# Moving the fourth recurrent head ahead of keys, values and queries in a hybrid encoder layer

## The chip, the cores and the metric

The kernel computes one encoder layer on one core of a Trainium2 chip. Its engines each run their own queue of instructions in order and meet at semaphores: TensorE (PE; its weight loads are shown as PEld), VectorE (DVE), ScalarE (ACT), GpSimd (POOL), and SyncE (SP), which issues transfers. The metric is the time of one execution in microseconds on the device (us); lower is better. Every time in this document is in us unless it says otherwise.

## The reference, cut to what matters

The layer has 512 tokens of width 1024 and a memory of 256 tokens. The change lies in the first sub-layer alone, which mixes tokens by two head groups side by side:

```
h = rmsnorm(x, pre_mix_g)
aq, ak, av, hq, hf_fwd, hf_bwd, hi, hg = split_columns(h @ w_in, (512, 128, 128, 512, 512, 512, 512, 512))
aq = rmsnorm(aq per head, q_norm_g);  ak = rmsnorm(ak per head, k_norm_g)
att = axial_gqa_attention(apply_rope(aq), apply_rope(ak), av)      # 8 heads of 64, 2 of keys and values
rec = hgrn2_group(hq, hf_fwd, hf_bwd, hi, hg, lb, hg_out_norm_g)   # 4 heads, gated scan in both directions
x = x + rmsnorm(concat(att, rec) @ w_out, post_mix_g)
m = rmsnorm(mem, mem_norm_g)
x = x + rmsnorm(memory_cross_attention(rmsnorm(x, pre_x_g), m, wq, wkv, wo), post_x_g)
x = x + rmsnorm(conv_ffn(rmsnorm(x, pre_ffn_g), ...), post_ffn_g)
```

Attention is softmax(q k / 8) v for each of the 8 heads. A recurrent head runs a scan with a forget gate forwards and backwards over the tokens, adds both, normalizes the sum and multiplies it by silu(hg).

## The kernel before, in words

**Products.** Every large product is made of three fp32r products of a high and a low part (`mm3`: hi·hi, hi·lo, lo·hi; lines 149, 150 and 151). So each operand has to be split into `hi` and `lo` first: ACT casts (line 103 or 126) and DVE subtracts (line 104).

**Weights.** The host packs all weights into 132 units of 128x1024. SP loads a unit into one of two `raw` buffers, ACT casts it into `wh` (line 126 for units 7 to 41), and the remainder `wl` follows in one of three ways: by DVE; by ACT and an accumulating transfer issued by POOL (units 7 to 27); or by a POOL multiplication (line 130) and such a transfer (line 131, units 28 to 41). `wh` and `wl` have four buffers each and a unit is asked for three units ahead, so that the cast of unit u+4 waits until PE has done the last product with unit u.

**The recurrent heads.** For head h, `hgrn_in(h)` projects three units (the query and two gates) feature-major into bank "b", each 24 products of 512 columns, and DVE scales each result (line 451). `hgrn_core(h)` then runs the scan as a chain of levels: PE makes four small products of a level (line 516), ACT and DVE (line 542) scale the keys and queries in place, and the next level needs that. At its end come the outputs (lines 554 to 556), their squares (ACT, line 560), a reciprocal root of four values per row by POOL (lines 167, 168), the gated scaling by DVE (line 566), four transposes on PE (line 570) and a split into the mixing operand.

**Queries.** The query projection leaves four blocks of 128 tokens in the banks "s" and "o". For each, `put_qn` squares (ACT, line 593), sums (DVE, line 595), makes eight reciprocal roots per row (POOL, lines 167, 168 and 597), turns by the rotary tables (DVE, lines 602 to 606), scales (line 607), splits (ACT line 103, DVE line 104), and transposes on PE (line 637, four transposes twice). A block's work is called a job below.

**Order.** Generators yield after each piece of work, and `weave` advances the one that is behind by its share; a tile scheduler then sets each engine's final order. First stage: `mix_projections` (gates, the memory's norm, heads 1 and 2, the memory's transposes `mem_turn`, keys and values, queries, head 3) with a share of 100 beside the cores of heads 0, 1 and 2 with a share of 53. The four jobs on the queries are called between the projections of head 3. Second stage: the core of head 3, `attention` (32 steps of scores, softmax, transposes and, every second step, products with the values, line 733) and `attention_filler`: the memory's keys as eight chunks of 24 products of 256 columns (units 26 to 33, one unit each), its values (units 34 to 37), and the first half of the output projection (units 38 to 41), in which the last unit waits for the last attention heads.

Of the kernel before, what the change touches and what calls it, by code (L numbers as in the profile page):

```python
# [31 lines left out]
TURN_STEP, MEM_TURN, UP_TURN = 0, (0, 4), (0, 2)  # L32
NEG_SCALAR = frozenset(range(7, 28))
NEG_POOL = frozenset(range(28, 42))
CORE_SHARE = 53.0
WARM, SPREAD_STEP = 4, 2
LEVELS = (1, 2, 4, 8, 16, 32, 64)
ASK = 3
# [35 lines left out]
def layer(tc, io, out):  # L74
# [18 lines left out]
    def big(shape, dt=F32):  # L93
        return b8.tile(shape, dt, name="big", tag="big")
# [366 lines left out]
                                       op0=ALU.mult, op1=ALU.mult)  # L461
        sg_box.append(b)

    def hgrn_in(h, between=()):
        qk = big([P, 2, 2, T])
        tt = big([P, 2048])
        q = tmp2(tag="tq")

        def put_q(z):
            nc.scalar.activation(q, z, ACT.Sigmoid)  # L470
            nc.vector.tensor_mul(q, z, q)

        def put_f(d):
            def put(z):
                f = tt[:, d * T:(d + 1) * T]
                k = qk[:, 1, d, :]
                nc.scalar.activation(f, z, ACT.Sigmoid)
                nc.scalar.activation(k, z, ACT.Sigmoid, scale=-1.0)
                nc.scalar.activation(f, f, ACT.Identity, scale=oml[:, d, h:h + 1], bias=lb[:, d, h:h + 1])
                nc.vector.scalar_tensor_tensor(out=qk[:, 0, 1 - d, :], in0=f, scalar=oml[:, d, h:h + 1], in1=q,  # L480
                                               op0=ALU.mult, op1=ALU.mult)
            return put

        for put in (put_q, put_f(0), put_f(1)):
            yield from proj_fm(hT, T, "b", scaled(put))
            for job in between[:2]:
                job()
            between = between[2:]
        heads[h] = (q, qk, tt)

    def hgrn_core(h):
# [118 lines left out]
    def put_kv(b, z):  # L610
        if "rope" not in qkv:
            qkv["rope"] = rope_tables()
            qkv["kT"] = big([P, 4, T], F32R)
            qkv["vv"] = const.tile([P, NB, 2, 2, 64], F32R, name="vv")
            qkv["qT"] = [big([P, 4, T], F32R) for _ in range(2)]
        vv = qkv["vv"]
        split_scaled(vv[:, b, :, 0, :], vv[:, b, :, 1, :], z[:, 128:256].rearrange("p (h d) -> p h d", h=2), r[:, b:b + 1])
        kr = norm_rope(z[:, 0:128], 2, 1, b)
        kd = tmp2((P, 2, 2, 2, 64), F32R)
        nc.scalar.copy(kd[:, :, 0], kr[:, :, None, :].to_broadcast([P, 2, 2, 64]))  # L620
        nc.vector.tensor_tensor(out=kd[:, :, 1], in0=kr[:, :, None, :].to_broadcast([P, 2, 2, 64]),
                                in1=kd[:, :, 0].bitcast(F32), op=ALU.subtract)
        o = bank("b").rearrange("p (k n) -> p k n", k=4)
        kd4 = kd.rearrange("p a b c d -> p (a b) (c d)")
        for i in range(4):
            nc.tensor.transpose(o[:, i, :].bitcast(F32R), kd4[:, i, :], ident_r)
        nc.scalar.copy(qkv["kT"][:, :, blk(b)], o)

    def put_qn(b, z):
        qr = norm_rope(z, 8, 0, b)  # L630
        qs = tmp4([P, 8, 2, 64], F32R)
        split(qs[:, :, 0, :], qs[:, :, 1, :], qr)
        q3 = qs.rearrange("p h a d -> p h (a d)")
        for g in range(2):
            o = bank("so"[g]).rearrange("p (k n) -> p k n", k=4)
            for i in range(4):
                nc.tensor.transpose(o[:, i, :].bitcast(F32R), q3[:, 4 * g + i, :], ident_r)
            if g:
                nc.vector.tensor_copy(qkv["qT"][g][:, :, blk(b)], o)
            else:  # L640
                nc.scalar.copy(qkv["qT"][g][:, :, blk(b)], o)
# [20 lines left out]
    def mix_projections():  # L662
        yield from proj_tm(hT, tm_tags, put_sg)
        mem_norm()
        yield from hgrn_in(1)
        yield from hgrn_in(2)
        mem_turn()
        yield from proj_tm(hT, tm_tags, put_kv, 256)
        late = []
        yield from proj_tm(hT, tm_tags, lambda b, z: late.append(lambda: put_qn(b, z)))  # L670
        yield from hgrn_in(3, late)

    def cores():
        for h in range(3):
            yield from hgrn_core(h)

    for i, _ in enumerate(hgrn_in(0)):
        if i == SPREAD_STEP:
            spread_r()
    weave((mix_projections(), 100.0), (cores(), CORE_SHARE))  # L680

    kT, vv, qT = qkv["kT"], qkv["vv"], qkv["qT"]

    scaled = [0]

# [18 lines left out]
    def attention():  # L704
        probs, pts, atts = {}, {}, {}

        def scores(i):
            h, qb = divmod(i, 4)
            s = bank("s")
            for c in range(2):  # L710
                nc.tensor.matmul(s, qT[h // 4][:, h % 4, blk(qb)], kT[:, 2 * (h // 4) + c, :],  # L711
                                 start=c == 0, stop=c == 1)
            probs[i] = softmax(s, 1, 512)

# [29 lines left out]
                att_done[0] += 1  # L744

        n = 8 * NB
        for i in range(n + 4):
            if i < n:
                scores(i)
            if 2 <= i <= n + 1:  # L750
# [25 lines left out]
        yield from proj_tm(kv["m"], "bb", put_vx(0))  # L776
        kv["y0"] = yield from res_first(mix, MIX_ORDER, lambda j: rec_done[0] == 4 if j >= 2 else att_done[0] >= 2 * j + 2)

    weave((hgrn_core(3), 22.0), (attention(), 42.0), (attention_filler(), 52.0))

    x = load_x()
    g_post, g_pre = gains("post_mix_g", "pre_x_g")
# [153 lines left out]
def pack_weights(w_in, w_xkv, w_out, w_xq, w_xo, w_up, w_down):  # L936
# [16 lines left out]
    tm(w_in, 2816)  # L953
    head(1)
    head(2)
    kv = w_in[:, 512:768].reshape(KC, P, 256)
    for j in range(2):
        units.append(kv[4 * j:4 * j + 4].transpose(1, 0, 2).reshape(P, 1024))
    tm(w_in, 0)
    head(3)  # L960
    for c in range(8):
        fm(w_xkv, c * P)
    tm(w_xkv, 1024)
# [59 lines left out]
```

## Time and profile before

| | |
|---|---|
| Median of three runs | 844.49 |
| Lowest, highest | 843.57, 844.58 |
| Profiled execution, time | 846.16 |
| Profiled execution, span | 844.3 |
| PE busy in the span | 828.5 (98%) |
| DVE, ACT, POOL busy | 488.2 (58%), 427.7 (51%), 102.4 (12%) |
| Mean granted PE clock | 0.996 |

The span is the stretch that the profiler shows on the core; 1.86 of the profiled execution's time lies outside it. Start times are from the span's start. "Granted clock" is the share of full speed at which PE was let run. In a row of the timeline stand start, duration, engine, line, operation, what it writes and reads, how many instructions are joined in the row (x4), and in brackets how long the engine stood idle before it and which engine's result ended that. The durations of pipelined products overlap: the distance between two starts says what one costs. A busy PE may still run its products further apart than it could, so that distances between starts also show waits that the idle time doesn't list.

The stage that the change touches goes from about 50 to 320. The query projection ends at 182, head 3's projections fill 182 to 198.7, and the memory's keys begin there.

### The profile page before, as it was taken

What the parts mean: (1) busy time and instruction counts of PE and PEld (TensorE: products, weight loads), DVE (VectorE), ACT (ScalarE), POOL (GpSimd) and SP (SyncE); (2) the same over time, 40 slices, a digit from 0 to 9 for tenths busy, and PEclk for the clock granted to TensorE, in tenths of its full rate; (3) what the DMA queues carried; (4) which work ended last, traced back from release to release, by engine and by line L of the source; (5) the groups of instructions that cost most, each with busy time, mean ns of one, the idle gap of its engine ahead of it and who ended that gap; (6) DMA issues with size and microseconds to landing.
All of it is one profiled execution on the core that took longest, in us unless ns stands there. A gap on an engine that the chain in (4) does not pass through costs nothing.

```text
span 844.3 us, 11078 instructions
## 1 busy us (share of the span) xinstructions
PE 828.5 (98%) x4304; PEld 703.4 (83%) x4304; DVE 488.2 (58%) x759; ACT 427.7 (51%) x736; POOL 102.4 (12%) x163
## 2 busy tenths in 40 slices
PE   9999999997999999999999999999999999999996
PEld 7888888886999888888888998888888888888885
DVE  5364677619996775854444865555555557722224
ACT  6576656546898874645443553333333335511121
POOL 0212202317223201300001300000000000000001
PEclk9999999999999999999999999999999999999999
DMA  9687754477477643341302333322222222322312
GB/s 322 182 202 203 159 112 113 101 153 181 98 157 162 149 131 119 101 160 65 125 25 75 99 126 101 101 95 88 93 99 99 100 101 94 101 88 94 99 50 100
DMA packets 29796, 101.81 MB, mean 121 GB/s; under 512 B 3952, under 2 KB 4464, under 8 KB 29744
## 3 DMA queue, kind: packets, MB, share of 16 engines
q1 hardware_dynamic: 22752, 77.38, 27.3%
q0 software_dynamic: 6272, 22.81, 14.7%
q10 hardware_dynamic: 720, 0.92, 0.3%
q8 instruction: 34, 0.56, 0.3%
q14 instruction: 18, 0.15, 0.1%
HBM read 99.00 MB, written 2.10 MB: 120 GB/s over the span
## 4 chain that ended last, share of the span: by engine, by line
PE 91%; DVE 3%; ACT 2%; DMA 2%; POOL 1%; issue 1%; POOLq 0%; DVEq 0%; ACTq 0%
PE ps_b L149 9%; PE ps_b L150 9%; PE ps_b L151 9%; PE ps_s L151 6%; PE ps_s L149 6%; PE ps_s L150 6%; PE ps_o L149 6%; PE ps_o L151 6%; PE ps_o L150 6%; PE ps_c L149 4%; PE ps_c L150 4%; PE ps_c L151 4%; PE ps_c L516 3%; PE ps_o L733 2%; PE ps_s L711 2%; PE ps_o L721 2%
## 5 line engine op out<-in xcount | busy, mean ns | idle before, releaser
L104 DVE TENSOR_TENSOR wl<-raw,wh 128x1024 fp32r<-128x1024 f32 x93 | 113.8, 1224 | 199.9 <-ACT wh L103 199.8
L103 ACT CAST wh<-raw 128x1024 fp32r<-128x1024 f32 x93 | 97.9, 1053 | 206.2 <-PE ps_o L151 71.4
L149 PE MATMUL ps_b<-big,wh 128*128 128x512 f32 (+1 forms) x320 | 118.6, 371 | 2.1 <-DVE tmp L451 2.1
L150 PE MATMUL ps_b<-big,wh 128*128 128x512 f32 (+1 forms) x320 | 117.5, 367 | 0.0
L151 PE MATMUL ps_b<-big,wl 128*128 128x512 f32 (+1 forms) x320 | 117.3, 367 | 0.0
L149 PEld LDWEIGHTS ps_b<-big,wh 128*128 128x128 f32 x320 | 61.0, 191 | 11.3 <-DVE tmp L451 2.3
L151 PEld LDWEIGHTS ps_b<-big,wl 128*128 128x128 f32 x320 | 60.9, 190 | 9.3
L150 PEld LDWEIGHTS ps_b<-big,wh 128*128 128x128 f32 x320 | 60.9, 190 | 9.0
L177 POOL TENSOR_SCALAR small<-small 128x1 f32<-128x1 f32 x40 | 13.9, 348 | 440.7 <-ACT tmp L208 421.8
L149 PE MATMUL ps_s<-wh,big 128*128 128x512 f32 (+1 forms) x140 | 54.1, 387 | 0.0
L151 PE MATMUL ps_s<-wh,big 128*128 128x512 f32 (+1 forms) x140 | 53.3, 381 | 0.0
L150 PE MATMUL ps_s<-wl,big 128*128 128x512 f32 (+1 forms) x140 | 53.0, 379 | 0.0
L542 DVE TENSOR_TENSOR big<-big 128x512 f32<-128x512 f32 x64 | 47.9, 755 | 8.4 <-PE ps_c L516 4.6
L126 ACT CAST wh<-raw 128x1024 fp32r<-128x1024 f32 x35 | 36.7, 1048 | 30.3 <-PE ps_o L151 16.1
L149 PE MATMUL ps_o<-wh,big 128*128 128x512 f32 (+1 forms) x124 | 47.9, 386 | 0.0
L151 PE MATMUL ps_o<-wh,big 128*128 128x512 f32 (+1 forms) x124 | 46.7, 377 | 0.0
L150 PE MATMUL ps_o<-wl,big 128*128 128x512 f32 (+1 forms) x124 | 46.7, 377 | 0.0
L131 POOL DMA_DIRECT2D wl<-in_w_dram x35 | 31.2, 892 | 112.9 <-ACT wl L128 103.3
L104 DVE TENSOR_TENSOR big<-ps_o,big 128x512 fp32r<-128x512 f32 x52 | 35.7, 688 | 15.1 <-ACT big L103 14.9
L103 ACT CAST big<-ps_o 128x512 fp32r<-128x512 f32 x52 | 30.3, 586 | 19.6 <-PE ps_o L830 7.5
L149 PE MATMUL ps_b<-wh,big 128*128 128x512 f32 x92 | 36.7, 399 | 0.0
L150 PE MATMUL ps_b<-wl,big 128*128 128x512 f32 x92 | 36.2, 393 | 0.0
(248 smaller groups left out, 1949.2 us busy)
## 6 DMA issues: line engine op xcount, KB each, us to landing
raw<-in_w_dram SPq DMA_DIRECT2D x131, 512.0 KB, 3.3
wl<-in_w_dram POOLq DMA_DIRECT2D x35, 512.0 KB, 5.6
big<-in_x_dram SPq DMA_DIRECT2D x8, 512.0 KB, 7.5
big<-in_xt_dram SPq DMA_DIRECT2D x3, 512.0 KB, 7.8
big<-in_mem_dram POOLq DMA_DIRECT2D x2, 512.0 KB, 8.2
out_dram<-big SPq DMA_DIRECT2D x4, 256.0 KB, 2.0
out_dram<-big ACTq DMA_DIRECT2D x3, 256.0 KB, 2.0
big<-in_xt_dram SPq DMA_DIRECT2D x2, 256.0 KB, 3.5
```

The source lines that it names most:

```text
L103: nc.scalar.copy(hi, src)
L104: (eng or nc.vector).tensor_sub(lo, src, hi.bitcast(F32))
L126: nc.scalar.copy(wh, raw)
L131: nc.gpsimd.dma_start(wl, io["w"][i], accum_op=ALU.add)
L149: nc.tensor.matmul(o, a[0], b[0], start=start, stop=False)
L150: nc.tensor.matmul(o, a[0], b[1], start=False, stop=False)
L151: last_mm[0] = nc.tensor.matmul(o, a[1], b[0], start=False, stop=stop).ins
L516: nc.tensor.matmul(o[:, b, :], kc[:, blk(b)], pat(qk, b * P, [[2 * m, P // (2 * m)], [T + m, 2], [1, m]]), start=True, stop=True)
L542: nc.vector.tensor_tensor(out=c, in0=c, in1=pat(tt, toff + off, [[2, npair], [gap, 2], [0, m]]), op=ALU.mult)
L711: nc.tensor.matmul(s, qT[h // 4][:, h % 4, blk(qb)], kT[:, 2 * (h // 4) + c, :], start=c == 0, stop=c == 1)
L721: nc.tensor.transpose(o[:, c, :], e[:, 0, blk(c)], ident)
L733: nc.tensor.matmul(o, vv[:, c, h // 4].rearrange("p a d -> p (a d)"), pt[:, j, c, :], start=c + j == 0, stop=c == 3 and j == 1)
```

## The change

Four things are moved. `mix_projections` projects head 3 right after heads 1 and 2, ahead of `mem_turn`, keys, values and queries, and the host packs the units in that order (units 17 to 19 are head 3's now, 20 and 21 keys and values, 22 to 25 queries; 26 and above are as they were). All four cores are woven beside the projections, with a share of 60 in place of 53, and so the second stage has none. The jobs on the queries become a stream of their own in the second stage (a share of 110, 3 per job), beside attention (47 in place of 42) and its filler (52). And attention begins with a lead of 5 on its stream, and each of its first four steps waits until as many jobs have been asked for. The transposes of a job go to bank "c" (the cores' bank) in place of "s" and "o", and the tiles for the transposed queries are taken when the first job runs. Lines of the changed kernel stand one lower than before up to `hgrn_in`'s head, then two higher (542 is now 540, 566 is 564), and `put_qn`'s transposes are line 636.

```diff
--- before.py
+++ after.py
@@ -32,7 +32,8 @@
 TURN_STEP, MEM_TURN, UP_TURN = 0, (0, 4), (0, 2)
 NEG_SCALAR = frozenset(range(7, 28))
 NEG_POOL = frozenset(range(28, 42))
-CORE_SHARE = 53.0
+CORE_SHARE = 60.0
+Q_STEP, ATT_LEAD = 3.0, 5.0
 WARM, SPREAD_STEP = 4, 2
 LEVELS = (1, 2, 4, 8, 16, 32, 64)
 ASK = 3
@@ -461,7 +462,7 @@
                                        op0=ALU.mult, op1=ALU.mult)
         sg_box.append(b)
 
-    def hgrn_in(h, between=()):
+    def hgrn_in(h):
         qk = big([P, 2, 2, T])
         tt = big([P, 2048])
         q = tmp2(tag="tq")
@@ -483,9 +484,6 @@
 
         for put in (put_q, put_f(0), put_f(1)):
             yield from proj_fm(hT, T, "b", scaled(put))
-            for job in between[:2]:
-                job()
-            between = between[2:]
         heads[h] = (q, qk, tt)
 
     def hgrn_core(h):
@@ -612,7 +610,6 @@
             qkv["rope"] = rope_tables()
             qkv["kT"] = big([P, 4, T], F32R)
             qkv["vv"] = const.tile([P, NB, 2, 2, 64], F32R, name="vv")
-            qkv["qT"] = [big([P, 4, T], F32R) for _ in range(2)]
         vv = qkv["vv"]
         split_scaled(vv[:, b, :, 0, :], vv[:, b, :, 1, :], z[:, 128:256].rearrange("p (h d) -> p h d", h=2), r[:, b:b + 1])
         kr = norm_rope(z[:, 0:128], 2, 1, b)
@@ -627,12 +624,14 @@
         nc.scalar.copy(qkv["kT"][:, :, blk(b)], o)
 
     def put_qn(b, z):
+        if "qT" not in qkv:
+            qkv["qT"] = [big([P, 4, T], F32R) for _ in range(2)]
         qr = norm_rope(z, 8, 0, b)
         qs = tmp4([P, 8, 2, 64], F32R)
         split(qs[:, :, 0, :], qs[:, :, 1, :], qr)
         q3 = qs.rearrange("p h a d -> p h (a d)")
         for g in range(2):
-            o = bank("so"[g]).rearrange("p (k n) -> p k n", k=4)
+            o = bank("c").rearrange("p (k n) -> p k n", k=4)
             for i in range(4):
                 nc.tensor.transpose(o[:, i, :].bitcast(F32R), q3[:, 4 * g + i, :], ident_r)
             if g:
@@ -664,22 +663,29 @@
         mem_norm()
         yield from hgrn_in(1)
         yield from hgrn_in(2)
+        yield from hgrn_in(3)
         mem_turn()
         yield from proj_tm(hT, tm_tags, put_kv, 256)
-        late = []
         yield from proj_tm(hT, tm_tags, lambda b, z: late.append(lambda: put_qn(b, z)))
-        yield from hgrn_in(3, late)
+
+    late, asked_q = [], [0]
 
     def cores():
-        for h in range(3):
+        for h in range(4):
             yield from hgrn_core(h)
+
+    def query_jobs():
+        while late:
+            late.pop(0)()
+            asked_q[0] += 1
+            yield Q_STEP
 
     for i, _ in enumerate(hgrn_in(0)):
         if i == SPREAD_STEP:
             spread_r()
     weave((mix_projections(), 100.0), (cores(), CORE_SHARE))
 
-    kT, vv, qT = qkv["kT"], qkv["vv"], qkv["qT"]
+    kT, vv = qkv["kT"], qkv["vv"]
 
     scaled = [0]
 
@@ -708,7 +714,7 @@
             h, qb = divmod(i, 4)
             s = bank("s")
             for c in range(2):
-                nc.tensor.matmul(s, qT[h // 4][:, h % 4, blk(qb)], kT[:, 2 * (h // 4) + c, :],
+                nc.tensor.matmul(s, qkv["qT"][h // 4][:, h % 4, blk(qb)], kT[:, 2 * (h // 4) + c, :],
                                  start=c == 0, stop=c == 1)
             probs[i] = softmax(s, 1, 512)
 
@@ -744,7 +750,10 @@
                 att_done[0] += 1
 
         n = 8 * NB
+        yield ATT_LEAD
         for i in range(n + 4):
+            while asked_q[0] < min(NB, i + 1):
+                yield None
             if i < n:
                 scores(i)
             if 2 <= i <= n + 1:
@@ -776,7 +785,7 @@
         yield from proj_tm(kv["m"], "bb", put_vx(0))
         kv["y0"] = yield from res_first(mix, MIX_ORDER, lambda j: rec_done[0] == 4 if j >= 2 else att_done[0] >= 2 * j + 2)
 
-    weave((hgrn_core(3), 22.0), (attention(), 42.0), (attention_filler(), 52.0))
+    weave((query_jobs(), 110.0), (attention(), 47.0), (attention_filler(), 52.0))
 
     x = load_x()
     g_post, g_pre = gains("post_mix_g", "pre_x_g")
@@ -953,11 +962,11 @@
     tm(w_in, 2816)
     head(1)
     head(2)
+    head(3)
     kv = w_in[:, 512:768].reshape(KC, P, 256)
     for j in range(2):
         units.append(kv[4 * j:4 * j + 4].transpose(1, 0, 2).reshape(P, 1024))
     tm(w_in, 0)
-    head(3)
     for c in range(8):
         fm(w_xkv, c * P)
     tm(w_xkv, 1024)
```

**PE where the second stage begins.** Around a job's transposes (line 637 before, 636 after; `tmp4` is the split query block, `ps_b` a chunk of the memory's keys, `wh` and `wl` its unit). Before, the third job's:

```order
L149 MATMUL ps_b_1888<-big_1110,wh_1647 128x256
L150 MATMUL ps_b_1888<-big_1111,wh_1647 128x256
L151 MATMUL ps_b_1888<-big_1110,wl_1648 128x256
L637 MATMUL ps_s_1790<-ident_r_262,tmp4_1787 128x128 x4
L637 MATMUL ps_o_1796<-ident_r_262,tmp4_1787 128x128 x4
L149 MATMUL ps_b_1942<-big_1110,wh_1739 128x256
L150 MATMUL ps_b_1942<-big_1111,wh_1739 128x256
```

After, the fourth job's:

```order
L150 MATMUL ps_b_2129<-big_1365,wh_1928 128x256
L151 MATMUL ps_b_2129<-big_1366,wh_1928 128x256
L152 MATMUL ps_b_2129<-big_1365,wl_1929 128x256
L636 MATMUL ps_c_2057<-ident_r_262,tmp4_2054 128x128 x4
L636 MATMUL ps_c_2063<-ident_r_262,tmp4_2054 128x128 x4
L150 MATMUL ps_b_2197<-big_1365,wh_1990 128x256
L151 MATMUL ps_b_2197<-big_1366,wh_1990 128x256
L717 MATMUL ps_s_2143<-big_1513,big_1894 128x512 x2
```

Before, the first job's transposes begin within head 3's last projection, the third's stand between the chunks of units 26 and 27 (above), and the fourth's within unit 27's. After, the first job's stand behind 27 products of the chunks of units 26 and 27, and those of the fourth (above) behind the four chunks of units 26 to 29, 96 products, with the first two pairs of score products (line 717) among them.

**POOL around the same jobs.** Lines 167, 168 and 597 (168, 169 and 595 after) are a job's reciprocal root, 130 and 131 (131 and 132) a unit's multiplication and transfer. Before, the third and fourth job:

```order
L167 TENSOR_SCALAR small_1778<-small_1776 128x8
L168 TENSOR_TENSOR small_1778<-small_1778,nhalf_82 128x8
L597 TENSOR_SCALAR small_1778<-small_1778,rx_276 128x8
L130 TENSOR_SCALAR wl_1892<-wh_1891 128x1024
L131 DMA wl_1892<-in_w_dram 128x1024
L167 TENSOR_SCALAR small_1806<-small_1804 128x8
L168 TENSOR_TENSOR small_1806<-small_1806,nhalf_82 128x8
L597 TENSOR_SCALAR small_1806<-small_1806,rx_276 128x8
L130 TENSOR_SCALAR wl_1946<-wh_1945 128x1024
L131 DMA wl_1946<-in_w_dram 128x1024
```

After:

```order
L168 TENSOR_SCALAR small_2005<-small_2003 128x8
L169 TENSOR_TENSOR small_2005<-small_2005,nhalf_82 128x8
L131 TENSOR_SCALAR wl_1991<-wh_1990 128x1024
L595 TENSOR_SCALAR small_2005<-small_2005,rx_276 128x8
L132 DMA wl_1991<-in_w_dram 128x1024
L131 TENSOR_SCALAR wl_2081<-wh_2080 128x1024
L168 TENSOR_SCALAR small_2045<-small_2043 128x8
L132 DMA wl_2081<-in_w_dram 128x1024
L169 TENSOR_TENSOR small_2045<-small_2045,nhalf_82 128x8
L595 TENSOR_SCALAR small_2045<-small_2045,rx_276 128x8
```

The number of instructions is the same; the third and fourth jobs' three now have multiplications and transfers of the units between them.

**PE at the end of head 1's core.** Line 556 (554 after) is the last product of the outputs, 570 (568) the transposes of the scaled outputs, 506 (504) the first product of the next core. Before, with the memory's transposes (line 193) and the keys and values (`ps_s`) between:

```order
L193 MATMUL ps_b_1126<-ident_79,big_720 128x128 x4
L151 MATMUL ps_s_1140<-wh_872,big_109 128x256
L570 MATMUL ps_c_1167<-ident_79,tmp2_1063 128x128 x4
L506 MATMUL ps_c_1178<-tmp2_868,tmp2_1175 128x128 x4
L149 MATMUL ps_s_1141<-wh_872,big_107 128x256
```

After, with head 3's projections between:

```order
L152 MATMUL ps_b_1083<-big_108,wl_832 128x512
L150 MATMUL ps_b_1083<-big_108,wh_831 128x512
L568 MATMUL ps_c_1076<-ident_79,tmp2_1025 128x128
L151 MATMUL ps_b_1083<-big_110,wh_831 128x512
L568 MATMUL ps_c_1076<-ident_79,tmp2_1025 128x128 x2
L152 MATMUL ps_b_1083<-big_108,wl_832 128x512
L568 MATMUL ps_c_1076<-ident_79,tmp2_1025 128x128
L150 MATMUL ps_b_1124<-big_107,wh_872 128x512
```

Between the last output product and the first transpose there stand 23 products and three groups of four memory transposes before, and 9 products after.

**DVE at the same place.** Line 566 (564) is the gated scaling, 451 (452) the scaling of a projection, 480 (481) a gate, 502 (500) the first instruction of the next core, 109 the split of the transposed outputs, 104 the split of the memory's transposes. Before:

```order
L542 TENSOR_TENSOR big_739<-big_739,big_740 128x2x2x128 x2
L480 SCALAR_TENSOR_TENSOR big_866<-big_867,oml_307,tmp2_868 128x512
L566 SCALAR_TENSOR_TENSOR tmp2_1063<-ps_c_1050,small_1069,big_653 128x128 x4
L451 TENSOR_TENSOR tmp2_1104<-ps_b_1072,big_292 128x512
L104 TENSOR_TENSOR big_1111<-ps_b_1112,big_1110 128x4x128
L502 SCALAR_TENSOR_TENSOR tmp2_1175<-big_866,oml_307,tmp2_1175 128x512
L480 SCALAR_TENSOR_TENSOR big_866<-big_867,oml_307,tmp2_868 128x512
```

After:

```order
L540 TENSOR_TENSOR big_739<-big_739,big_740 128x2x2x128 x2
L481 SCALAR_TENSOR_TENSOR big_866<-big_867,oml_307,tmp2_868 128x512
L564 SCALAR_TENSOR_TENSOR tmp2_1025<-ps_c_1012,small_1031,big_659 128x128 x4
L452 TENSOR_TENSOR tmp2_1115<-ps_b_1083,big_292 128x512
L109 SCALAR_TENSOR_TENSOR big_771<-ps_c_1076,og_296,big_771 128x512
L500 SCALAR_TENSOR_TENSOR tmp2_1139<-big_866,oml_307,tmp2_1139 128x512
L481 SCALAR_TENSOR_TENSOR big_866<-big_867,oml_307,tmp2_868 128x512
```

The next core's first instruction now stands behind the split of the outputs of the core before.

## The prediction

> **What bounds the kernel now.** I read the page's busy times first, then PE's waits and the stretches of the stage that changes, then its timeline.
>
> ```profile
> PE 828.5 (98%) x4304; PEld 703.4 (83%) x4304; DVE 488.2 (58%) x759; ACT 427.7 (51%) x736; POOL 102.4 (12%) x163
> ```
>
> PE bounds the span, so an edit is worth what it takes from, or adds to, PE's gaps. In PE's waits between 100 and 260 (us in total, times, longest) and in two stretches of 25 (PE first, granted clock third from the end):
>
> ```profile
> PE ps_s L637 <- DVE tmp L104: 2.5, 2, 1.9
> PE ps_b L149 <- DVE tmp L451: 2.1, 1, 2.1
> PE ps_c L516 <- DVE big L542: 1.2, 2, 1.0
> PE ps_b L193 <- DVE tmp L451: 0.8, 1, 0.8
> PE ps_o L733 <- DVE big L104: 0.5, 1, 0.5
> ...
> 125.00:150.00 25.00, 23.11 (x179) 21.87 (x178) 18.63 (x42) 15.73 (x33) 4.89 (x9) 1.00 0.42 96
> 200.00:225.00 25.00, 20.97 (x152) 19.98 (x153) 23.21 (x41) 20.26 (x37) 8.86 (x11) 0.93 0.52 114
> ```
>
> The worst stretch is 200 to 225, where the query jobs, head 3's core and the start of attention all want DVE (23.21 of 25). The timeline of PE there, and the clock in steps of 3:
>
> ```profile
> 181.99 0.39 PE L149 MATMUL ps_b<-big,wh 128*128 128x512 f32 x1
> ...
> 203.21 0.28 PE L150 MATMUL ps_b<-big,wh 128*128 128x256 f32 x1
> 203.33 0.28 PE L151 MATMUL ps_b<-big,wl 128*128 128x256 f32 x1
> 205.50 0.54 PE L637 MATMUL ps_s<-ident_r,tmp 128*128 128x128 f32 x4 [1.89 <-DVE tmp L104]
> 208.50 0.38 PE L149 MATMUL ps_b<-big,wh 128*128 128x256 f32 x1 [2.12 <-DVE tmp L451]
> 209.10 0.42 PE L149 MATMUL ps_b<-big,wh 128*128 128x256 f32 x1
> 209.32 0.41 PE L150 MATMUL ps_b<-big,wh 128*128 128x256 f32 x1
> ...
> 206.00:209.00 3.00, 0.88 (x8) 0.74 (x7) 3.00 (x6) 1.11 (x2) 1.98 (x3) 0.96 0.99 239
> 209.00:212.00 3.00, 3.00 (x16) 3.00 (x16) 2.38 (x5) 2.59 (x5) 0.00 (x0) 0.50 0.95 182
> ```
>
> A 256-column product costs 0.12 (203.21 to 203.33), at the half clock that follows the two waits 0.22 (209.10 to 209.32). Some 15 go at half clock: 1.4 lost.
>
> **What the change takes away.** The first two rows of the waits and the last all hang on DVE's load in this stage; head 3's core leaves it, and nothing is projected beside the jobs. That is 2.5 + 2.1 + 0.5 = 5.1. By distances between starts the two long waits are 0.3 larger than their brackets, the short one ahead of them 0.1. With the clock's 1.4: −6.9.
>
> **What the jobs cost in their new place.** They now start at the end of the query projection (t = 0, 181.99 in the old trace), and PE has only the memory's keys to fill with. One job's chain before, and the price of its links:
>
> ```profile
> 189.07 0.69 DVE L595 TENSOR_REDUCE small<-tmp 128x8 f32<-128x512 f32 x1 [0.75 <-ACT tmp L593]
> ...
> 189.85 0.57 POOL L167 TENSOR_SCALAR small<-small 128x8 f32<-128x8 f32 x1 [4.35 <-DVE small L595]
> ...
> 193.81 0.19 POOL L167 TENSOR_SCALAR small<-small 128x8 f32<-128x8 f32 x1
> 194.08 1.66 POOL L168 TENSOR_TENSOR small<-small,nhalf 128x8 f32<-128x8 f32 x1
> 195.85 0.63 POOL L597 TENSOR_SCALAR small<-small,rx 128x8 f32<-128x8 f32 x1
> 196.44 1.07 POOL L130 TENSOR_SCALAR wl<-wh 128x1024 fp32r<-128x1024 f32 x1
> 197.81 0.92 POOL L131 DMA_DIRECT2D wl<-in_w_dram  x1 [0.30 <-POOL wl L130]
> 198.80 0.19 POOL L167 TENSOR_SCALAR small<-small 128x8 f32<-128x8 f32 x1
> ...
> L607 DVE TENSOR_TENSOR tmp<-tmp,small x4: 674/927/1533, 193.3 to 208.4; 128x512 f32<-128x512 f32 x4
> ...
> 182.19 1.05 ACT L126 CAST wh<-raw 128x1024 fp32r<-128x1024 f32 x1 [3.21 <-PE ps_o L151]
> ...
> wl<-in_w_dram POOLq DMA_DIRECT2D x7, 512.0 KB, 5.9
> ```
>
> A job's three POOL instructions take 2.63 (193.81 to 196.44), the first job's 3.0; a unit's multiplication and transfer 2.36 (196.44 to 198.80). Block 0 leaves PE 4 ahead of t = 0, so POOL begins at about −2.2: jobs one and two are done at 3.5. Unit 29's cast can't start before t = 0 (the 182.19 row is the same wait), so its 2.36 stands next, and POOL is at 5.9. Then, in the order's words, the third job's three with unit 30's multiplication among them (2.6 + 1.1, 9.7 with the gap), unit 30's transfer (11.0), unit 31's multiplication (12.1), the fourth job's first, unit 31's transfer (13.4), and the fourth's other two: 15.75. DVE follows with the scaling (1.2, between L607's 0.67 and 1.53, since a multiplication of POOL runs beside it), two maxima of scores that stand ahead in its queue (0.6 each), and the remainder: the last job's transposes can start at 18.95.
>
> PE reaches them at 96 × 0.119 = 11.4, plus three earlier jobs' transposes at 0.7 (2.1; a group of four starts 0.4 behind the other), four score products at 0.23 (0.9) and 0.3 for changes between kinds: 14.7. All its waits up to there are 18.95 − 14.7 = +4.25: 0.3 at the first job, about 1 at the third, the rest, 2.6 to 2.9, at the fourth. Behind the waiting transposes PE's queue holds unit 30's products and the next scores, and ACT and DVE then wait for these, so that nothing hides it. The transfers of units 29 and 30, issued at 5.0 and 10.1, land 5.9 later (the last row), at 10.9 and 16.0; PE wants them behind the third job's transposes (13.5) and the fourth's (19.6). Behind the fourth job, up to the memory's values, the ordered instructions at their old durations add to 26.9 for ACT and 26.4 for PE: within each other's slack, so I take no wait there, and price the opposite as a rival.
>
> The clock is the unknown: before, it halved after 4.9 without a large product (203.5 to 208.5). The new long wait with its 0.7 of transposes makes 3.3 to 3.6. The bounds are 0 and +1.4 (the halving before). I take 0, since this is two thirds of the stretch that halved it and the first wait of 1.89 alone left the clock at full (0.96 over 206 to 209, 0.50 only behind).
>
> The Trainium skill (TensorE: Matmul & The Clock Gate, sections What's actually happening, Why this matters for your kernels, and Part 4: PE-mode transpose) says that PE shouldn't idle for more than about 3 us, that the gate looks at a window of some 3.4 us that runs freely, and that transposes don't count as work. By the first of these the clock would halve and the sum be 846.6, by the window it may just not. The trace agrees for the old drop (4.9 without a product) and shows no stretch between 3 and 4.
>
> **Heads 1 and 2.** The end of head 1's core, whose links do not depend on what runs beside it:
>
> ```profile
> 126.08 0.47 PE L150 MATMUL ps_b<-big,wh 128*128 128x512 f32 x1
> ...
> 128.95 1.13 DVE L566 SCALAR_TENSOR_TENSOR tmp<-ps_c,small,big 128x128 f32<-128x128 f32 x4 [5.30 <-POOL small L168]
> ```
>
> From the end of the last output product to the first quarter of L566's 1.13 are 3.26 (126.08 to 129.23 and a handover). Before, 23 products and 12 memory transposes cover it; now 9 products at 0.24 (2.16): +1.1. Bounds: 0, if the order's single products between the four transposes absorb the wait, and 3.3, if nothing covers; I take the row's.
>
> Head 2's core now starts among head 3's projections, as head 1's did among head 2's:
>
> ```profile
> 102.20 0.40 PE L151 MATMUL ps_b<-big,wl 128*128 128x512 f32 x1
> 102.59 1.59 PE L516 MATMUL ps_c<-big,tmp 128*128 128x128 f32 x8
> 103.88 0.54 PE L149 MATMUL ps_b<-big,wh 128*128 128x512 f32 x1
> 104.26 0.39 PE L150 MATMUL ps_b<-big,wh 128*128 128x512 f32 x1
> ...
> 104.72 0.39 PE L149 MATMUL ps_b<-big,wh 128*128 128x512 f32 x1
> 104.94 0.39 PE L150 MATMUL ps_b<-big,wh 128*128 128x512 f32 x1
> 105.52 0.72 PE L516 MATMUL ps_c<-big,tmp 128*128 128x128 f32 x4 [0.19 <-DVE big L542]
> ```
>
> A product of 512 columns costs 0.22 (104.72 to 104.94), and eight small ones as much work as about 0.8; here 1.29 go by; 103.88 to 104.26 and 104.94 to 105.52 are 0.16 and 0.36 over a product's, and 0.2 more lies ahead: 1.2, though PE shows as busy. For head 2 the split of the transposed outputs stands ahead of its first instruction on DVE, a tenth more: +1.3. Head 3's core takes over what head 2's met beside keys, values and queries (1.2 at L516, 0.8 at L193): net 0, within ±0.8. DVE has the room: 18.63 of 25 there. PE changes between fp32 and fp32r operands 108 times in the new order against 105; at 0.1 each, below the 0.17 by which 102.20 to 102.59 exceeds a product and above nothing, that is +0.3.
>
> **The end of attention.** The last split of attention feeds the output projection:
>
> ```profile
> 317.41 0.40 PE L149 MATMUL ps_b<-wh,big 128*128 128x512 f32 x1
> ...
> 319.35 0.62 ACT L103 CAST big<-tmp 128x512 fp32r<-128x512 f32 x1 [1.36 <-DVE tmp L739]
> ...
> 320.02 0.50 PE L149 MATMUL ps_b<-wh,big 128*128 128x512 f32 x1
> ```
>
> 317.41 to 320.02 is 2.61, covered before by 11 products; the new order leaves 8 (1.85): +0.7.
>
> Costed at nothing: bank "c", since the last core's transposes stand 52 rows ahead of the first job's in PE's order; the query tile taken later, as no one asks for its slot between; the three units packed earlier, since units 17 to 25 all take the same path (ACT twice, a POOL transfer) and SP issues as many transfers, with three units ahead to cover the 5.9 of one; the lead of attention, since its steps stand where the fillers want them. If that cover fails at one unit, it costs up to 5.9 less the three units' products, which are 16: nothing.
>
> **Sum.** −6.9 + 4.25 + 0 + 1.1 + 1.3 + 0.3 + 0.7 = +0.75. The profiled execution (846.16, span 844.3) would come to 846.9 and 845.05; it stands 1.67 above the median of the runs, so on the median: 844.49 + 0.75 = 845.2. A measurement of this kernel can tell about 0.2%, ±1.7, from no change, so this counts as no change.
>
> **Rivals.**
> 1. The clock halves again behind the fourth job: 846.6. For it: the old drop, in the same place. Against: a shorter stretch.
> 2. The jobs come in time: faster. If the fourth job's transposes can start within 15.2 of t = 0 rather than 18.95, only 0.5 of the 4.25 stays: 841.5. The point from which it decides is 3.75 off the chain; units 30 and 31's instructions, ahead of the fourth job on POOL, are worth 2 × 2.36 = 4.7. For it: in the old trace the jobs waited for DVE (the brackets at 205.50 and 208.50), which now has less to do. Against: ACT's casts came as soon as PE let them, and the order puts their POOL work ahead.
> 3. The POOL chain is later by 1.5: multiplications and transfers disturbed (the L607 row's 1.53 twice, maxima waiting for scores); the stretch is then near 4.9 and the clock halves: +1.5 + 1.4: 848.1, slower.
> 4. ACT becomes the bound of attention. With head 3's core gone, ACT needs 26.9 to PE's 26.4; at 0.2 per step over 11 steps: 847.4, slower. For it: 20.26 of 25 busy before with the core's share among it; against: it streamed without waits after 231.
>
> **How the numbers follow.** My forecast 0.28; rival 1 0.20; rival 2 0.21; rival 3 0.09; rival 4 0.12; 0.10 for what I haven't named, of both signs. Their values reach from 841.5 to 848.1; 0.5 more on each side takes in the ±0.8 of the heads: 841.0 to 848.6. The forecast alone, with ±0.8 for the heads and ±1 for the fourth job, is 843.4 to 847.0. Faster by over 0.2%: rival 2 (0.21), 0.04 of the forecast's lower end, 0.03 unnamed: 0.28. Within: 0.17 of the forecast, 0.07 of rival 1, 0.02: 0.26. Slower: 0.07, 0.13, rivals 3 and 4 (0.21), 0.05: 0.46.
>
> **What would show it.** In the new trace PE's waits should show L636 behind DVE's split with 2.6 to 2.9 once and about 1 once, and no wait of bank "b" behind L452; a clock of 1.00 behind the long one (0.50 for rival 1). L568 of head 1 should wait 1.1. PE's busy time in the 25 before the query projection's end should be near that of 125 to 150. If no L636 waits above 1, rival 2 holds; if score products wait for ACT in steps of 0.2, rival 4. Wrong altogether would be a wait that I took as covered, at the transfers of units 29 and 30 above all.

## The result and the profile after

| | before | after |
|---|---|---|
| Median (4 runs each) | 844.54 | 853.95 |
| Lowest, highest | 843.57, 845.46 | 849.62, 854.47 |
| Span of the profiled execution | 844.3 | 852.7 |
| PE busy in the span | 828.5 | 832.1 |
| Mean granted PE clock | 0.996 | 0.994 |

The changed kernel is slower: the ratio of its runs to those of before is 1.0096, with a 95% interval of 1.008 to 1.0112. The forecast was 845.2 in a range of 841.0 to 848.6, so it missed by 8.8, and the median lies 5.35 beyond the range.

The waits of PE after the change, between 40 and 340 (engine, what it waited for, total, times, longest):

```profile
PE ps_c L568 <- DVE tmp L564: 5.3, 2, 4.3
PE ps_c L636 <- DVE tmp L105: 3.9, 2, 2.4
PE ps_b L194 <- DVE tmp L452: 1.0, 1, 1.0
PE ps_c L514 <- DVE big L540: 1.0, 3, 0.4
PE ps_c L504 <- DVE tmp L500: 0.5, 1, 0.5
PE ps_o L739 <- DVE big L105: 0.4, 2, 0.2
```

The old waits at the handover (transposes behind the jobs' split, a chunk behind L451) are gone, and L636 stands in their place with 3.9, as forecast. The first row is the surprise: of its 5.3, 1.0 is head 1's end, which the prediction has; 4.3 is head 0's end, which it doesn't. The stretches of 25 in which PE is idle, and where its clock falls (first PE, third from the end the clock), show the same two places:

```profile
75.00:100.00 25.00, 20.73 (x100) 17.08 (x99) 9.26 (x16) 12.04 (x24) 6.99 (x12) 0.93 0.72 186
...
225.00:250.00 25.00, 21.10 (x158) 19.80 (x158) 19.14 (x37) 17.27 (x33) 13.80 (x15) 0.93 0.74 166
```

Before, PE lost nothing between 75 and 100 (25.00 busy at clock 1.00). Now the chain there, in order of time over four engines:

```profile
76.23 1.39 POOL L651 DMA_DIRECT2D big<-in_mem_dram  x2
...
80.60 0.69 ACT L460 ACTIVATE tmp<-ps_o,rx 128x512 f32<-128x512 f32 x1 [0.24 <-PE ps_o L152]
85.28 1.06 ACT L203 ACTIVATE tmp<-big 128x1024 f32<-128x1024 f32 x1 [3.99 <-DMA big<-in_mem_dram]
...
86.33 0.67 ACT L460 ACTIVATE tmp<-ps_o,rx 128x512 f32<-128x512 f32 x1
...
87.37 0.75 DVE L185 SCALAR_TENSOR_TENSOR big<-big,small 128x512 f32<-128x512 f32 x1 [4.52 <-POOL small L169]
88.04 0.75 DVE L461 SCALAR_TENSOR_TENSOR big<-ps_o,rx,tmp 128x512 f32<-128x512 f32 x1
88.70 2.07 DVE L185 SCALAR_TENSOR_TENSOR big<-big,small 128x512 f32<-128x512 f32 x3
90.68 0.35 DVE L564 SCALAR_TENSOR_TENSOR tmp<-ps_c,small,big 128x128 f32<-128x128 f32 x1
...
86.42 0.39 PE L151 MATMUL ps_b<-big,wh 128*128 128x512 f32 x1
91.08 0.33 PE L568 MATMUL ps_c<-ident,tmp 128*128 128x128 f32 x1 [4.27 <-DVE tmp L564]
...
91.95 0.62 PE L152 MATMUL ps_b<-big,wl 128*128 128x512 f32 x1
92.37 0.63 PE L150 MATMUL ps_b<-big,wh 128*128 128x512 f32 x1
```

Line 203 is the square of the first block of the memory's rows, 460 and 461 make the gate of a token block, 185 scales the memory's rows, and 564 multiplies head 0's output by the gate. The memory's square stands ahead of the last gate block in ACT's queue and waits for a transfer until 85.28. ACT runs in order: the products of that gate block end at 81.9, and its row starts only behind the square, at 86.33. DVE runs in order too: it has a scaling of the memory's rows ahead of the last gate block (88.04), and three more (88.70) ahead of the last quarter of L564 (90.68). PE's last transpose of head 0 waits for that. PE then runs eight to nine products at half clock, 0.43 apart (91.95 to 92.37). By starts, 86.42 to 91.08 is 4.43 more than a product, and the half clock costs 1.6 to 1.8: some 6.1 in all, of 8.4 by which the spans differ (the medians differ by 9.4).

In the old trace the two memory squares stood behind all four gate blocks and behind the core's own squares. ACT in the kernel before:

```profile
78.74 0.69 ACT L459 ACTIVATE tmp<-ps_o,rx 128x512 f32<-128x512 f32 x1 [0.70 <-PE ps_o L151]
...
82.56 1.06 ACT L202 ACTIVATE tmp<-big 128x1024 f32<-128x1024 f32 x1
```

78.74 is the last gate block, and the square at 82.56 finds its rows there. What swapped them is the cores' share: with 60 in place of 53, head 0's core ends 12 products earlier in PE's order (56 in place of 68 stand between its first products and its outputs). The core's squares now stand ahead of the last two gate blocks on ACT, and the memory's first square ahead of the last one. Why the scheduler then moves the memory's square as well isn't shown; that the share does it, the runs below show.

### The profile page after: what moved, and what is told of

It is laid out like the page before. It is cut to its first block, busy times and chain, and to the rows that moved or that the text cites. A ratio compares the mean times of both kernels' runs of the same rounds, so it can differ in the third digit from the quotient of the medians.

```text
span 852.7 us, 11091 instructions
## 1 busy us (share of the span) xinstructions
PE 832.1 (98%) x4304; PEld 702.5 (82%) x4304; DVE 489.1 (57%) x759; ACT 426.8 (50%) x736; POOL 102.6 (12%) x163
## 4 chain that ended last, share of the span: by engine, by line
PE 89%; ACT 3%; POOL 3%; DVE 2%; DMA 2%; issue 1%; POOLq 0%; DVEq 0%; ACTq 0%
PE ps_b L152 9%; PE ps_b L150 9%; PE ps_b L151 9%; PE ps_s L152 6%; PE ps_s L151 6%; PE ps_s L150 6%; PE ps_o L150 6%; PE ps_o L151 6%; PE ps_o L152 6%; PE ps_c L151 4%; PE ps_c L150 4%; PE ps_c L152 4%; PE ps_c L514 4%; PE ps_o L739 2%; PE ps_o L727 1%; PE ps_s L717 1%
```

## The experiments

All times are medians; "before" in each set is the kernel before on the same chip: 845.48 for the first four runs (the share alone, the share back to 53, the transfers earlier, the norm later); 844.3 for head 0 at its old pace (alone, with units 28 to 31, and with these and the longer pause) and for these units with the early transfers; 844.72 for the second measurement, these units on the kernel before, and head 1's pause; 844.8 for the last. Each ratio is to the kernel before of its own set, so that runs of different sets are better compared by ratios than by medians.

**The share alone, on the kernel before.**

```diff
-CORE_SHARE = 53.0
+CORE_SHARE = 60.0
```

> The kernel before with one number changed: the cores' share is 60 in place of 53; head 3 stays where it was. Theory (T1: the share alone moves the first square of the memory, which waits for the memory's transfer, ahead of the last gate block on ScalarE, and so holds up head 0's last quarter): the wait of some 4 us at head 0's transposes and the half clock behind it show here too, about +6: 850.5. Rival (T2: the wait comes of head 3's new place, by the load on the engines beside it): no wait at head 0's end, 844 to 845.5.

Measured: 854.85, ratio 1.0112 (1.0093 to 1.0131). PE's waits and the two stretches with a lower clock:

```profile
PE ps_c L570 <- DVE tmp L566: 4.2, 2, 3.1
PE ps_s L637 <- DVE tmp L104: 2.5, 2, 1.9
PE ps_b L149 <- DVE tmp L451: 2.1, 1, 2.1
PE ps_c L523 <- DVE big L542: 1.3, 1, 1.3
...
75.00:100.00 25.00, 21.87 (x108) 18.14 (x107) 9.22 (x16) 13.36 (x26) 7.01 (x12) 0.93 0.72 186
200.00:225.00 25.00, 20.42 (x119) 18.32 (x119) 22.27 (x34) 15.14 (x24) 16.13 (x19) 0.86 0.75 162
```

The wait at head 0's end is there without moving any head: one number does it, and the rival T2 falls. The number costs this kernel more than the 6 expected, since it disturbs more: a wait of 1.3 in head 2's levels, 1.05 at head 1's end, and the old handover with the clock at 0.86 rather than 0.93.

**The share back to 53 on the changed kernel.**

```diff
-CORE_SHARE = 60.0
+CORE_SHARE = 53.0
```

> The changed kernel with the cores' share back at 53, everything else as changed. T1: no wait at head 0's end, 853.9 less 6: 847.5 to 848.5. T2: the wait stays within 1 us, 853 to 854.5. What is left above 844.5 is then the price of the rest of the change; the prediction's terms give 845.2, or 846.6 with the clock halved behind the fourth query job.

Measured: 851.44, ratio 1.0069 (1.0055 to 1.0083): 3 above the band of T1. PE has 25.00 between 75 and 100 again, so the wait is gone, but the slower cores pay at the other end:

```profile
PE ps_c L636 <- DVE tmp L105: 4.6, 2, 2.3
PE ps_b L623 <- ACT tmp L617: 1.4, 2, 0.7
...
225.00:250.00 25.00, 22.67 (x154) 21.34 (x154) 18.91 (x41) 17.64 (x37) 7.26 (x9) 0.85 0.43 95
```

The last core ends among the first query jobs (its transposes wait until 214), and the jobs' waits then halve the clock for longer (0.85). So four cores beside the projections need the faster pace at their end, and head 0 needs the slower one at its own.

**The memory's transfers earlier, and its norm later.** Two ways to take away what ACT waits for, with the share at 60. In the first, `mem_load` takes the gain's and the rows' transfers out of `mem_norm`, and stands ahead of the gate projection:

```diff
+        mem_load()
         yield from proj_tm(hT, tm_tags, put_sg)
         mem_norm()
```

> The changed kernel with the memory's transfers (gain and rows) issued ahead of the gate projection in place of behind it; share 60 stays, and the squares still stand between the gate blocks. T1: ScalarE's first square finds its data, the 4.3 us wait at head 0's last quarter falls below 1 and with it the half clock: 847 to 848.5. If the order alone (not the transfer) made the wait, it stays above 2: 850 to 854.

Measured: 849.81, ratio 1.0051 (1.0038 to 1.0065). PE's wait, and ACT where it waited:

```profile
PE ps_c L568 <- DVE tmp L564: 1.7, 2, 1.0
...
81.28 1.08 ACT L203 ACTIVATE tmp<-big 128x1024 f32<-128x1024 f32 x1
...
82.32 1.37 ACT L460 ACTIVATE tmp<-ps_o,rx 128x512 f32<-128x512 f32 x2
```

The longest wait at L568 is 1.0 now (head 1's), head 0's is 0.6, and the clock stays full between 75 and 100. The square even stands ahead of the last two gate blocks here (82.32), and with its data there it does little harm: the transfer's landing was the cause, as T1 has it. The whole edit is worth 4.1 by the medians (3.8 by the ratios), and more than head 0's end is in that: the waits at the jobs' transposes come to 2.4 in place of 3.9, and head 0's start is later (50 to 75: 23.15 of 25 busy, against 24.07 in the changed kernel). That 0.9 is most of the 1.3 by which it comes out above the band. In the second, the norm is placed behind head 1's projections:

```diff
-        mem_norm()
         yield from hgrn_in(1)
+        mem_norm()
```

> The changed kernel with the memory's norm placed behind head 1's projections, so that the last gate block stands ahead of it on ScalarE and VectorE. T1: no wait at head 0's end, 847 to 848.5. If the late part is head 0's chain itself (squares, roots on GpSimd) and not the memory's, the wait stays: 852 to 854.

Measured: 851.42, ratio 1.007 (1.0058 to 1.0082). PE has 25.00 between 75 and 100, so T1 holds at that place, but the time misses its band by 3, for the wait moved. ACT a little later, and PE's wait there:

```profile
106.50 1.06 ACT L203 ACTIVATE tmp<-big 128x1024 f32<-128x1024 f32 x1 [3.02 <-DMA big<-in_mem_dram]
...
PE ps_c L514 <- ACT tmp L511: 3.2, 1, 3.2
```

Here the second square waits 3.0 for its transfer, ahead of a level of head 1's core (L511, L514), and the clock halves there (0.93 between 100 and 125).

**Head 0's core at its old pace, the others at 60.** `H0_SLOW` is 60/53:

```diff
         for h in range(4):
-            yield from hgrn_core(h)
+            for step in hgrn_core(h):
+                yield step * H0_SLOW if step and h == 0 else step
```

> The changed kernel in which head 0's core alone advances as before (each of its steps counts 60/53 as much), while heads 1 to 3 keep the share of 60. The order at head 0's end is then that of before (all four gate blocks ahead of the memory's squares) and the last core still ends ahead of the queries. If the wait at head 0's end and its half clock are all that share 60 does wrong: 853.9 less 6, 847.5 to 848.5. If the faster head 0 also cost something at its start (the first 1.5 between 50 and 75): 846 to 847.5. If later cores slip by it: above 849.

Measured: 844.55, ratio 0.9998 (0.9987 to 1.0008): as fast as before, 9.4 below the changed kernel and better than any of the bands. More than head 0's end comes back: as the cores shift, 33 products rather than 24 stand between the third job and the fourth in PE's order. The waits at the handover, and the clock, are:

```profile
PE ps_b L151 <- DVE big L106: 2.6, 2, 1.4
PE ps_c L637 <- DVE tmp L106: 0.6, 2, 0.3
...
200.00:225.00 25.00, 23.28 (x160) 21.05 (x158) 16.62 (x28) 12.27 (x25) 17.14 (x22) 1.00 0.71 159
225.00:250.00 25.00, 23.50 (x182) 21.91 (x182) 20.63 (x45) 22.80 (x48) 9.46 (x9) 1.00 0.74 162
```

(Lines stand one higher in this kernel: 637 is the jobs' transposes.) It is the cleanest look at the move of head 3 itself that these runs give, with the share of 60 still on heads 1 to 3: without its effect on head 0, the change neither gains nor loses.

**What the jobs wait for.** Units 28 to 31 are negated by ACT in place of POOL, on the kernel with the early transfers, on the kernel with head 0 slowed, and on the kernel before:

```diff
-NEG_SCALAR = frozenset(range(7, 28))
-NEG_POOL = frozenset(range(28, 42))
+NEG_SCALAR = frozenset(range(7, 32))
+NEG_POOL = frozenset(range(32, 42))
```

> The changed kernel with the memory's transfers early, and units 28 to 31 negated by ScalarE in place of GpSimd, so that no unit's multiplication stands among the query jobs on GpSimd. Theory (T3: the jobs' waits on PE come of GpSimd's queue, which holds four multiplications among the roots): the waits at the job transposes fall from 2.4 to below 0.7 and the clock stays full there: 849.8 less 3 to 4, 845.5 to 847. Rival (T4: the roots and VectorE's seven passes per job set the pace): waits above 1.5 stay, 849 to 850. If ScalarE becomes late by its four more passes of 1.05: new waits behind it, 849 to 851.

Measured: 847.03, ratio 1.0025 (1.0014 to 1.0036); with the early transfers alone it was 849.81, ratio 1.0051. The waits at the jobs' transposes fall from 2.4 to 1.7 and the clock stays at 1.00 in every stretch of 25 between 50 and 325. That is T3 in the direction and at the edge of its band; the waits stay above the 0.7 that it named, so that the four multiplications are only part of them. They act in two ways: with them, DVE's scalings of the third and fourth job stood idle 0.95 and 1.39 for POOL, and the fourth job's took 1.51 beside a multiplication; without them neither waits for POOL, and they take 0.68 and 0.96.

> Both together without the early transfers: head 0's core at its old pace, and units 28 to 31 negated by ScalarE. If the two costs are apart and add: 843.5 to 845.5, about the kernel before. What would then be left against it are the ends and starts of heads 1 and 2 (+2.4 by the prediction) against the old handover's 6.9. If the terms overlap: 846 to 848.

Measured: 842.62, ratio 0.9979 (0.997 to 0.9989), below all bands given: faster than before by 0.2%. A second measurement of the same kernel was to tell chance from gain:

> The best combination unchanged, beside the two others on the same chip: 842.6, 0.2% below the kernel before. If the 0.2% was the chip's or the hour's: 844 to 845.

Measured: 842.82, ratio 0.9968 (0.9956 to 0.9981). The gain stays. But it isn't the moved head's:

> The kernel before with units 28 to 31 negated by ScalarE in place of GpSimd, nothing else. It tells whether the gain of the last combination belongs to that edit alone. If the old handover's waits come of VectorE's load, as its rows name it: 843.5 to 844.5, no gain beyond 0.1%. If GpSimd's queue set them as well: 841 to 843.

Measured: 842.09, ratio 0.9966 (0.9954 to 0.9979), the edit alone on the kernel before, and the fastest kernel of this study. PE's waits there:

```profile
PE ps_b L149 <- DVE tmp L451: 2.1, 1, 2.1
PE ps_s L637 <- DVE tmp L104: 1.4, 1, 1.4
PE ps_b L193 <- DVE tmp L451: 0.8, 1, 0.8
PE ps_c L516 <- DVE big L542: 0.6, 2, 0.4
```

L637's 2.5 of before is 1.4 and L733's 0.5 is gone. Their rows named DVE, and my expectation that DVE's load alone set them was wrong. But POOL's queue, which its second half names, isn't the cause here. The second and third job's scalings on DVE, in the kernel before and then with the edit:

```profile
196.51 1.53 DVE L607 TENSOR_TENSOR tmp<-tmp,small 128x512 f32<-128x512 f32 x1 [0.17 <-POOL small L597]
201.81 1.18 DVE L607 TENSOR_TENSOR tmp<-tmp,small 128x512 f32<-128x512 f32 x1
...
194.23 0.69 DVE L607 TENSOR_TENSOR tmp<-tmp,small 128x512 f32<-128x512 f32 x1 [0.17 <-POOL small L597]
198.81 0.68 DVE L607 TENSOR_TENSOR tmp<-tmp,small 128x512 f32<-128x512 f32 x1
```

In the kernel before they run beside multiplications of POOL (196.44 and 201.40) and take 1.35 longer in all. The third root on POOL starts at 198.80, right behind DVE's sum (which ends at 198.64), so that the multiplication ahead of it held it up by 0.2 at most. DVE was late, as its name in the rows says, since POOL's passes stretched two of its own. The 2.6 between the medians aren't all explained by that: in the two traces, 2.3 of the 4.0 between the spans stand ahead of these units, 1.25 of them where DVE waits 1.59 for the transfer of the rotary tables in the trace of before and not in the other (PE's 1.0 at L516 there).

**Head 1's end.** The price of its wait by giving it more cover, on the combination of 842.62, first for all heads:

```diff
-        yield 3.0
+        yield 4.5
```

> As the one before, with the pause of a core ahead of its gated scaling 4.5 in place of 3, so that 23 products stand between head 1's last output and its transposes in place of 9. If the wait at head 1's transposes costs its 1.2: 1 to 1.5 less than the one before, 842 to 844. If the later end of each core pushes the next one's start or the query jobs back: no gain or up to 3 slower.

Measured: 851.24, ratio 1.0081 (1.0063 to 1.0099): the later ends push the last core into the query jobs (job transposes wait 3.1, chunks 3.0, the clock is 0.82 between 225 and 250). Then for head 1 alone, with the later heads sped up to make good for it:

```diff
-        yield 3.0
+        yield 5.0 if h == 1 else 3.0
...
-                yield step * H0_SLOW if step and h == 0 else step
+                yield step * (H0_SLOW, 1.0, 0.85, 0.85)[h] if step else step
```

> The best combination so far (head 0's core at its old pace, units 28 to 31 negated by ScalarE) with a pause of 5 ahead of the gated scaling for head 1 alone and the later heads counted at 0.85, so that 17 products stand ahead of head 1's transposes and the last core still ends ahead of the query jobs. If the wait there costs its 1.2: 841.4, 1 to 1.4 less than 842.6. If the shifts it makes in the later heads cost as much: 842.3 to 844.

Measured: 843.40, ratio 0.9986 (0.9977 to 0.9995), against 842.82 without it on the same chip. The wait at head 1's transposes is gone from the list, and the jobs' is 1.7 where it was 0.6: what one place gives, another takes. Two numbers changed at once here, so that the price of head 1's wait alone isn't shown.

**The early transfers on the kernel before with a share of 60.**

> The kernel before with the share of 60 and, besides, the memory's transfers issued ahead of the gate projection. If the wait for the memory's transfer is what share 60 costs at head 0's end in either kernel, the wait of 3.1 there and its half clock go here too: 854.9 less 5, 849 to 850.5. The rest of the share's price on the kernel before (a wait of 1.3 at a level of head 2's core, starts and ends of cores) then stays. If the wait moves to another place, as in the kernel with the memory's norm later: 852 to 855.

Measured: 851.78, ratio 1.0081 (1.0067 to 1.0094), 3.1 below the same kernel with late transfers (2.6 by the ratios) and 1.3 short of the band. Head 0's wait falls below 1.0 and the clock is 1.00 between 75 and 100; the rest of the share's price stays (its 1.3 in head 2's levels, the clock of 0.86 at the handover), with 1.4 at head 0's start in place of 0.7.

## Why the prediction was wrong

**The step that failed: there was no term for head 0.** The sum went through heads 1, 2 and 3, the jobs and the end of attention. The share's step from 53 to 60 appears in none of its terms and is not among the things "costed at nothing" either. On PE the place looks covered, since 24 products still stand between head 0's outputs and its first transposes, as before. On ACT and DVE the memory's square and scalings had moved ahead of the last gate block, and the sum took that wait at nothing without a reason. The runs put in its place: some 6.1 by starts in the changed kernel, 4.1 between the medians with the early transfers, and 9.4 with head 0's core at its old pace. The list of what could go wrong altogether named "the transfers of units 29 and 30"; it was a transfer, but the memory's, 130 earlier.

**The other terms**, against the trace after:

- The old handover, −6.9: gone as forecast. But DVE's load isn't its whole cause: two of DVE's passes were stretched beside multiplications of POOL, and taking four of these off POOL on the kernel before brings L637's 2.5 to 1.4 with all of DVE's work still there.
- The jobs, +4.25 in waits: 3.9. The fourth job's transposes were to start 18.95 behind the end of the query projection:

```profile
219.88 0.39 PE L152 MATMUL ps_o<-wh,big 128*128 128x512 f32 x1
...
232.73 0.84 PE L636 MATMUL ps_c<-ident_r,tmp 128*128 128x128 f32 x8 [1.45 <-DVE tmp L105]
236.44 0.28 PE L152 MATMUL ps_b<-big,wl 128*128 128x256 f32 x1
239.16 1.23 PE L636 MATMUL ps_c<-ident_r,tmp 128*128 128x128 f32 x8 [2.45 <-DVE tmp L105]
240.19 0.54 PE L150 MATMUL ps_b<-big,wh 128*128 128x256 f32 x1
...
239.00:242.00 3.00, 2.84 (x14) 2.67 (x15) 1.28 (x5) 2.89 (x7) 0.00 (x0) 0.50 1.07 216
```

  The next piece of work starts at 220.11, and the transposes start at 239.16: 19.05. The third job waits 1.45 (about 1 forecast), the fourth 2.45 (2.6 to 2.9). This part of the working, added up link by link from old rows, held.
- The clock, taken as 0: it halved (last row), rival 1. Transposes and scores ran in that time beside products, so that it cost some 1.2, not 1.4.
- Head 1's end, +1.1: a wait of 1.04. It is the share's as well: the kernel before with a share of 60 waits 1.05 there, also behind 9 products, and the changed kernel with 53 has 17 products there and no wait. Head 2's start, +1.3: the rows from 141.39 to 145.64 in the new trace, which correspond to head 1's in the old one, exceed an undisturbed row by 1.4. Head 3 beside keys and queries, net 0: 1.0 at the memory's transposes for 0.8 before, but nothing for the 1.2 at L516, so −1.0. By the traces of the kernel before with and without POOL's multiplications (above), 1.0 of that 1.2 hung on the transfer of the rotary tables, not on the core.
- The end of attention, +0.7: no wait stands there; the first product that needs the last split comes late enough. Attention without head 3's core ran without waits for ACT; rival 4 was wrong, as was rival 2.

With −6.9, 3.9, 1.2, 1.0, 1.4, −1.0 and head 0's 6.1, and 0.5 at head 0's start, these terms make 6.2 of the spans' 8.4; 2.2 I haven't placed. Had head 0 stayed as it was, the forecast was close in its number: with its core at the old pace the changed kernel takes 844.55, against 845.2. That is luck in part: the jobs' transposes wait 0.6 there and not 4.25, and waits of 2.6 at the chunks, which the forecast doesn't have, stand in their place, at full clock.

Left open: one of the changed kernel's four runs took 849.62. Both kernels whose square waits for the transfer at head 0's end spread widely (849.62 to 854.47, and 851.77 to 856.98 for the share alone), and with early transfers they spread by 1.5 (848.61 to 850.07, 851.1 to 852.63). That would fit a landing time that varies; but the kernel with the norm later waits for a transfer too and spreads by 1.7 only, and two kernels without such a wait spread by 2.7 and 3.5 (the changed kernel at 53, and the longer pause). The granted clock tells more: it was 0.998 in the execution of 849.62 and 0.991 to 0.994 in the other three. Kernels whose clock stays at 1.00 in every stretch of 25 from 50 to 325 come to 0.998 as well (844.68 and 846.87, profiled), so that in this execution the clock seems to have halved at neither place; the two halvings are worth some 2.9 (1.7 and 1.2) of the 4.3 by which it lies below the median. Why they stayed away is open, as no trace of it was taken.

## What to carry to other kernels

When a constant that paces one stream against others is changed, compare the order on every in-order engine at every place where that stream meets another, also far from the edit's purpose: here ScalarE and VectorE at head 0's end, 130 ahead of the handover that the change is about. An instruction that waits for a transfer should not stand, in an in-order queue, ahead of work that the bounding engine waits for; issue the transfer earlier or keep the order. And the engine named behind a wait is the last link only: here DVE was named, and lightening POOL beside it (842.09 against 844.72) was worth more than the whole rearrangement.

## What the runs showed of the hardware that I had not expected

The clock halved after shorter stretches than I allowed for. In the kernel with early transfers, PE at the third job:

```profile
226.78 0.28 PE L152 MATMUL ps_b<-big,wl 128*128 128x256 f32 x1
228.54 0.85 PE L636 MATMUL ps_c<-ident_r,tmp 128*128 128x128 f32 x8 [1.48 <-DVE tmp L105]
229.39 0.38 PE L150 MATMUL ps_b<-big,wh 128*128 128x256 f32 x1
229.97 0.39 PE L151 MATMUL ps_b<-big,wh 128*128 128x256 f32 x1
230.15 0.41 PE L152 MATMUL ps_b<-big,wl 128*128 128x256 f32 x1
230.37 0.41 PE L150 MATMUL ps_b<-big,wh 128*128 128x256 f32 x1
```

A wait of 1.48 and eight transposes make 2.6 from one large product to the next (226.78 to 229.39), and from 230 on the products stand 0.22 apart. In the changed kernel the same stretch with the same wait (231.00 to 233.58, the wait of 1.45 at 232.73) left the clock at full, with products 0.12 apart behind it (233.80 to 233.92); the fourth job's 2.45 halved it, after 3.75 from one large product to the next (236.44 to 240.19). The forecast's reasoning that 3.3 to 3.6 is "two thirds of the stretch that halved it" was no ground for full clock. The Trainium skill (TensorE: Matmul & The Clock Gate, section What's actually happening) says that the gate looks at windows of about 3.4 us that run freely, which fits that the same stretch halves the clock once and not another time, though 2.6 is shorter than an idle window of 3.4.
